# One decoder layer on one core: sums of u read from DRAM, and the order of the pooling pairs on TensorE

## The chip, the cores and the metric

The kernel runs on one core of one Trainium2 chip. Its time is the device time of one execution in microseconds. All work of the layer is in one program; nothing is computed on the host, which only lays out the weights in blocks.

## What is computed

512 tokens and 16 learned meta tokens in front of them (528 columns), model width 1024, one layer, float32. The normalised input goes through one wide projection. Its parts feed a pooling branch, an SSD branch (state-space scan, 8 groups of 4 heads) and two gates. The gated sum goes through `w_o`, then a squared-ReLU MLP, then a last norm.

```python
u = rmsnorm(h, mix_norm_w[i]); proj = u @ w_in[i]
u_pool, z, xbc, dt_raw, gates = ...                       # columns of proj
y_pool = pool_mixer(u_pool, pool_w_group[i], pool_scale[i]) @ w_pool_up[i]
y_ssd = mamba2_branch(z, xbc, dt_raw, ...) @ w_ssd_out[i]
h = h + (gate_pool * y_pool + gate_ssd * y_ssd) @ w_o[i]
hid = relu(rmsnorm(h, mlp_norm_w[i]) @ w_ff1[i]); h = h + (hid * hid) @ w_ff2[i]
...
def pool_mixer(u, w_group, scale):                        # windows 2, 4, 8, 16 for 4 groups of 256 channels
    ...
        mean = (cs - shifted) / count
        outs.append(mean.astype(u.dtype) - xg)
    y = einsum("blgc,gcd->blgd", stack(outs), w_group); return y * scale
```

## The kernel before

Every matrix is kept as a high part and a low part in the fp32r type, and a product takes three matmuls: high with high, high with low, low with high. ScalarE (ACT) casts the high part and VectorE (DVE) subtracts it to get the low part. For weights this is done per block of 128 x 1024: a load on the SyncE queue into `raw` (3 buffers), then `whi` and `wlo` (4 buffers each), at lines 82 and 83. So each 24 matmuls of width 512 on TensorE (PE) need one block from ACT and one from DVE.

The program is written as Python generators and placed by a planner: each engine executes a fixed queue in order, and the planner, which follows the traced order as priority, decides that queue ahead of time. `tc.issue_after(ins)` puts all instructions that are traced inside it, on the engine of `ins`, behind `ins` in that engine's queue.

**Start.** `norm_u` (line 375) scales the transposed input `xt[k]`, 8 tiles of 128 x 528, to u and splits it into `uh[k]` and `ul[k]`. Then the memory of `xt` is given up, and tiles of the SSD stage take it.

**SSD groups.** `weave` runs, for each g of 8, the scan `ssd(g)` step by step beside the projections of group g+1 (`group_proj`); in group 4 also `out_half`, whose products `pso` are copied from PSUM to `acc` by ACT at line 615. `ssd(g)` begins with `abc_load[g]`, a broadcast of 1 MB on GpSimd's (POOL's) DMA queue into the single buffer `abc`; ACT reads it first into `eb` (line 483). The mask is applied at line 522 (`masked[g]`), the squares are taken at line 546.

**Sums of u.** The projections of three pooling groups use a Strassen-like scheme on halves of K and of the tokens. It needs sums and differences of pieces of u. `sums_of_u(k, g)` (line 636) makes them for k = 0 to 3 in groups g = 1 to 4: POOL adds `uh + ul` for tiles k and k+4 into `ua` and `ub` (line 641), DVE combines them (lines 644 to 647), and for each of two results, "13" and "42", ACT casts `th` (line 651), DVE subtracts `tl` (line 652), and both are stored to DRAM, to the tensors `t_d13h`, `t_d13l`, `t_d42h` and `t_d42l`, on POOL's queue (lines 653, 654). `th` and `tl` have one buffer each, so the cast of "42" waits until the store of "13" has read `th`.

**Pooling.** After the groups, the first pooling group (3, window 16) is projected directly. The others (2, 1, 0, in this order; windows 8, 4, 2) are made by `pool_pair(p)`: four weight forms A, S, D and B are split (`split_form`, lines 100 and 101), and seven products of 12 matmuls of width 260 run in the order A into x, A into y, S into x, S into z, D into x, D into z, B into x. Between them ACT copies x and z out (lines 735, 739, 741, 749) and DVE adds y, x and z (737, 744, 746) into the two result tiles `pu`, of which there are 2 buffers. `averaged` (line 687) then takes the moving mean on DVE (lines 694, 696) and splits it into `ph` (line 700) and `pl` (701). `pool_mix` multiplies the two means of a pooling group by its 256 x 256 matrix: 12 matmuls of width 512 into two `pg` tiles, read out by lines 762 and 763. In PSUM x of all pairs lies in one tile of two banks, `pxx`, in alternating banks, and y and z in another one, `pyz`. `pool_pair` is a generator that stops after the fourth product; there `pool_mix` of the pooling group before it is traced, and then the other three products.

**After that** come the SSD gates (`pgs`), the up-projection (`pup`), `w_o` and the MLP, which the change does not touch.

Of the kernel before, what the change touches and what calls it, by code (L numbers as in the profile page):

```python
# [9 lines left out]
F32 = mybir.dt.float32  # L10
F32R = mybir.dt.float32r
AF = mybir.ActivationFunctionType
ALU = mybir.AluOpType

P = 128
# [3 lines left out]
L = SEQ + NM  # L19
HALF = L // 2  # L20
NK = D // P
# [20 lines left out]
POOL_ORDER = (3, 2, 1, 0)  # L42
# [4 lines left out]

SKIP = 8
TN = (L - SKIP) // 2


@with_exitstack
def kernel(ctx: ExitStack, tc, xT, x, w, vec, fnw, out):
    nc = tc.nc
    act, dve, pe, pool = nc.scalar, nc.vector, nc.tensor, nc.gpsimd
# [3 lines left out]
    dram = ctx.enter_context(tc.tile_pool(name="dram", bufs=1, space=bass.MemoryType.DRAM))  # L59
# [25 lines left out]
    def block():  # L85
        t = block_tiles()
        block_part(t, slice(0, 1024))
        return t[2:]
# [48 lines left out]
    def col(off, i, n=P):  # L137
        return vs[:n, off + i : off + i + 1]
# [10 lines left out]
    uh = [up.tile([P, 64 + SEQ], F32R, name=f"uh{k}")[:, 64 - NM :] for k in range(NK)]  # L149
    ul = [up.tile([P, 64 + SEQ], F32R, name=f"ul{k}")[:, 64 - NM :] for k in range(NK)]  # L150
# [6 lines left out]
    def psum2(name):  # L157
        return psa.tile([P, 1024], F32, tag="mm", name=name)
# [35 lines left out]
    xt = [pre.tile([P, L], F32, name=f"xt{k}") for k in range(NK)]  # L194
# [177 lines left out]
    act.activation(fl(cdec), pq[:, :128], AF.Exp)  # L372


    def norm_u():
        for k in range(NK):
            dve.scalar_tensor_tensor(xt[k], xt[k], col(V_MIX, k), rsb, op0=ALU.mult, op1=ALU.mult)
            act.copy(uh[k], xt[k])
            dve.tensor_tensor(ul[k], xt[k], uh[k].bitcast(F32), op=ALU.subtract)

# [59 lines left out]
    def ssd(g, cur):  # L440
# [71 lines left out]
        for c in range(3):  # L512
            pe.matmul(pv[c + 1], btok[:, c, :], xdd[:, c, :, :].rearrange("p r d -> p (r d)"),
                      start=True, stop=True)
        st0 = act.copy(flat(st[0]), pv[0])
        if g == G - 1:
            with tc.issue_after(st0.ins):
                decay()
# [24 lines left out]
            yield  # L543

        sq = gs.tile([P, 2, SEQ], F32, tag="eb", name=f"sqg{g}")
        act.activation(sq, yt, AF.Square)
        dve.tensor_tensor(sq[:, 0, :], sq[:, 0, :], sq[:, 1, :], op=ALU.add)
        qh, ql = col_sums(f"g{g}", sq[:, 0, :], gs, ("qh", "ql"))
        yield
# [15 lines left out]
            ys.append((yh, yl))  # L565
        yield

    done, abc_load, masked = {}, {}, {}

    def weave(a, b, n):  # L570

# [64 lines left out]
    def sums_of_u(k, g):  # L636
        a, b = (tsp.tile([P, 2 * TN], F32, tag=t, name=f"{t}{k}") for t in ("ua", "ub"))

        with tc.issue_after(abc_load[g].ins):
            for t, kk in ((a, k), (b, k + 4)):  # L640
                pool.tensor_tensor(t, uh[kk][:, SKIP:L].bitcast(F32), ul[kk][:, SKIP:L].bitcast(F32), op=ALU.add)
        yield
        with tc.issue_after(masked[g].ins):
            dve.tensor_tensor(a[:, one], a[:, two], a[:, one], op=ALU.subtract)
            dve.tensor_tensor(a[:, two], b[:, two], a[:, two], op=ALU.subtract)
            dve.tensor_tensor(b[:, two], b[:, two], a[:, one], op=ALU.subtract)
            dve.tensor_tensor(b[:, one], b[:, one], b[:, two], op=ALU.subtract)
        yield
        for src, n in ((a, "13"), (b, "42")):
            hi, lo = (tsp.tile([P, 2 * TN], F32R, tag=f"t{p}", name=f"t{p}{n}{k}") for p in "hl")  # L650
            act.copy(hi, src)
            dve.tensor_tensor(lo, src, hi.bitcast(F32), op=ALU.subtract)
            nc.gpsimd.dma_start(t_d[n, "h", k], hi)
            nc.gpsimd.dma_start(t_d[n, "l", k], lo)
            yield

    for g in range(G):
        nxt = group_tiles(g + 1) if g + 1 < G else None
        fill = [group_proj(g + 1, nxt, GATE_AT.get(g))] if nxt else [out_part()]
        if g == 4:  # L660
            fill = [out_half()] + fill
        if 0 < g < 5:
            fill.append(sums_of_u(g - 1, g))
        weave(ssd(g, cur), fill, 2 if g == 4 else 1)
        cur = nxt
    gc_stack.close()
# [5 lines left out]
    pool_stack = ExitStack()  # L672
    gp = pool_stack.enter_context(tc.tile_pool(name="gp", bufs=2, side="left", reuse_waits="tile"))
    tf = pool_stack.enter_context(tc.tile_pool(name="tf", bufs=1, side="left", reuse_waits="tile"))
    yps = {}

    def pool_tile(t):
        win = WIN[t // 2]
# [9 lines left out]
    def averaged(t, u):  # L688
        win = WIN[t // 2]
        s, wdt, lo_ = u, 1, min(NM - win, NM - 4)  # L690
        while wdt < win:
            o = gp.tile([P, L], F32, tag="pw", name=f"pw{t}_{wdt}")
            lo2 = lo_ + wdt
            dve.tensor_tensor(o[:, lo2:], s[:, lo2:], s[:, lo_ : L - wdt], op=ALU.add)
            s, lo_, wdt = o, lo2, 2 * wdt
        dve.scalar_tensor_tensor(s[:, NM:], s[:, NM:], 1.0 / win, u[:, NM:],
                                 op0=ALU.mult, op1=ALU.subtract)
        ph = gp.tile([P, SEQ], F32R, tag="ph", name=f"ph{t}", bufs=3)
        pl_ = gp.tile([P, SEQ], F32R, tag="pl", name=f"pl{t}", bufs=3)
        act.copy(ph, s[:, NM:])  # L700
        dve.tensor_tensor(pl_, s[:, NM:], ph.bitcast(F32), op=ALU.subtract)
        return ph, pl_

    def pool_pair(p):

        a1, a2 = raw_block(), raw_block()
        sm = tf.tile([P, 1024], F32, tag="sm", name=f"sm{p}")
        h1, h2, both = slice(0, 512), slice(512, 1024), slice(0, 1024)
        fa = split_form(a1, both, f"A{p}")
        dve.tensor_tensor(sm[:, h1], a2[:, h1], a2[:, h2], op=ALU.add)  # L710
        dve.tensor_tensor(sm[:, h2], sm[:, h1], a1[:, h1], op=ALU.subtract)
        fs = split_form(sm, both, f"S{p}")
        dve.tensor_tensor(a1[:, h1], a1[:, h1], a2[:, h1], op=ALU.subtract)
        dve.tensor_tensor(a1[:, h2], a1[:, h2], sm[:, h2], op=ALU.subtract)
        fd = split_form(a1, both, f"D{p}")
        fb = split_form(a2, h2, f"B{p}")
        r1, r2 = (gp.tile([P, L], F32, tag="pu", name=f"pu{2 * p + i}") for i in range(2))
        n = POOL_ORDER.index(p) % 2
        x, y, z = pxx[:, 512 * n : 512 * n + TN], pyz[:, :TN], pyz[:, 512 : 512 + TN]
        c1, c2 = slice(SKIP, SKIP + TN), slice(SKIP + TN, L)  # L720
        u1, u2 = (lambda k: (uh[k][:, c1], ul[k][:, c1])), (lambda k: (uh[k][:, c2], ul[k][:, c2]))
        form = lambda n, c: lambda k: (T[n, "h", k][:, c], T[n, "l", k][:, c])

        def product(ps, wf, c, f, start, stop, k0=0):
            for low in range(2):
                for k in range(4):
                    wt = wf[low][:, 512 * c + k * P : 512 * c + (k + 1) * P]
                    bh, bl = f(k0 + k)
                    pe.matmul(ps, wt, bh, start=start and not low and k == 0, stop=stop and low == 1 and k == 3,
                              skip_group_check=True)  # L730
                    if not low:
                        pe.matmul(ps, wt, bl, start=False, stop=False, skip_group_check=True)

        product(x, fa, 0, u1, True, False)
        act.copy(r1[:, c1], x)
        product(y, fa, 1, u1, True, True, 4)
        dve.tensor_tensor(r1[:, c1], r1[:, c1], y, op=ALU.add)
        product(x, fs, 1, form("42", two), False, False)
        act.copy(r1[:, c2], x)
        product(z, fs, 0, form("13", one), True, False)  # L740
        act.copy(r2[:, c2], z)
        yield
        product(x, fd, 0, form("13", two), False, False)
        dve.tensor_tensor(r2[:, c2], r2[:, c2], x, op=ALU.add)
        product(z, fd, 1, u2, False, True, 4)
        dve.tensor_tensor(r1[:, c2], r1[:, c2], z, op=ALU.add)
        first = averaged(2 * p, r1)
        product(x, fb, 1, form("42", one), False, True)
        act.copy(r2[:, c1], x)
        yield [first, averaged(2 * p + 1, r2)]  # L750

    def pool_mix(gi, pooled, wgb):
        ps = [psum1(f"pg{gi}_{j}") for j in range(2)]
# [29 lines left out]
        dve.tensor_tensor(acc[d], acc[d], ps, op=ALU.add)  # L783
    wgb = block()
    gate_pool(NK - 1)
    pxx, pyz = psum2("pxx"), psum2("pyz")
    for n, gi in enumerate(POOL_ORDER):
        if n < 3:
            pair = pool_pair(POOL_ORDER[n + 1])
            next(pair)  # L790
        if n == 3:
            gts = [gate_ssd(MERGE[0])]
        if n == 2:
            wgb = block()
        pool_mix(gi, pend, wgb)
        if n < 3:
            pend = next(pair)
    pool_stack.close()
    wo_stack = ExitStack()
    wop = wo_stack.enter_context(tc.tile_pool(name="wop", bufs=1, side="right", reuse_waits="tile"))  # L800
# [389 lines left out]
    for t in range(4):  # L1190
        T, st = t // 2, slice((t % 2) * P, (t % 2 + 1) * P)
        n = 0
# [27 lines left out]
def _weight_blocks(i):  # L1220
# [5 lines left out]
    def cols(m, c):  # L1226
        a = m[:, c : c + P]
        return a.reshape(NK, P, P).transpose(1, 0, 2).reshape(P, NK * P)

    def put(b):  # L1230
        blocks.append(b)
# [35 lines left out]
    wg(POOL_ORDER[0] // 2)  # L1267
    gate(NK - 1)
    for n in range(4):
        if n < 3:  # L1270
            for i in range(2):
                put(cols(w_in, (2 * POOL_ORDER[n + 1] + i) * P))
        if n == 3:
            gate(NK + MERGE[0])
        if n == 2:
            wg(POOL_ORDER[n] // 2)
# [78 lines left out]
```

## Time and profile before

| what | value |
|---|---|
| runs | 1027.02, 1026.06, 1026.90 us; median 1026.9 |
| the profiled execution | 1030.26 us, of which the span from first to last instruction is 1028.5 us |
| mean granted TensorE clock | 0.994 |
| PE busy | 1010.4 us (98%), 5661 matmuls |
| DVE busy | 773.1 us (75%) |
| ACT busy | 559.0 us (54%) |
| POOL busy | 38.7 us (4%), 64 instructions |
| DMA | 114.15 MB, mean 111 GB/s |

How to read rows of a timeline: start in us, duration in us, engine, line, operation, result<-inputs, shape, count of merged instructions; in brackets the idle time of the engine just before, and what ended it. `PEld` is the loading of weights into TensorE. A row of windows has, for each stretch, its length and then the busy time and count of PE, PEld, DVE, ACT and POOL, the granted clock, the DMA share and GB/s.

### The profile page before, as it was taken

How to read it: one execution, taken by the hardware profiler on the slowest of the kernel's cores; microseconds unless marked ns; L12 is line 12 of the kernel's file. 1: busy time of each engine (PE TensorE's matmuls, PEld its weight loads, DVE VectorE, ACT ScalarE, POOL GpSimd, SP SyncE). 2: the span in 40 equal slices, each digit the busy share in tenths (PEclk: the TensorE clock that was granted, in tenths of full speed). 3: DMA queues.
4: the chain of work that ended last, by engine and by line, in shares of the span. 5: the costliest groups of instructions: out<-in, count | busy, mean ns of one | idle time of the engine just before them, and what ended most of it. 6: DMA issues, size and time to landing. Idle time of an engine off the chain costs nothing. (4 is left out here: it accounts for less than half of the span.)

```text
span 1028.5 us, 14191 instructions
## 1 busy us (share of the span) xinstructions
PE 1010.4 (98%) x5661; PEld 869.4 (85%) x5661; DVE 773.1 (75%) x1039; ACT 559.0 (54%) x746; POOL 38.7 (4%) x64
## 2 busy tenths in 40 slices
PE   9999999999989999999989999999999999999997
PEld 8889899898879998978888888888888888888886
DVE  7978798978826676988868467877686686676866
ACT  7674958585727439573245333365545455454444
POOL 0101011202000000003000000000000000000000
PEclk9999999999989999999999999999999999999999
DMA  7242142615233321417223632224323323334112
GB/s 249 80 158 82 63 144 84 201 42 189 82 103 124 103 81 64 144 41 238 93 82 128 221 91 98 119 76 170 92 81 114 110 85 117 100 101 123 42 42 82
DMA packets 34322, 114.15 MB, mean 111 GB/s; under 512 B 3856, under 2 KB 5200, under 8 KB 33232
## 3 DMA queue, kind: packets, MB, share of 16 engines
q1 hardware_dynamic: 26928, 92.75, 28.5%
q0 software_dynamic: 6608, 19.60, 5.6%
q8 instruction: 44, 0.72, 0.3%
q10 hardware_dynamic: 720, 0.91, 0.2%
q14 instruction: 22, 0.18, 0.1%
HBM read 106.81 MB, written 6.42 MB: 110 GB/s over the span
## 5 line engine op out<-in xcount | busy, mean ns | idle before, releaser
L82 ACT CAST whi<-raw 128x1024 fp32r<-128x1024 f32 (+1 forms) x128 | 130.3, 1024 | 180.9 <-PE pf L115 47.0
L83 DVE TENSOR_TENSOR wlo<-raw,whi 128x1024 fp32r<-128x1024 f32 (+1 forms) x128 | 153.9, 1206 | 99.4 <-ACT whi L82 63.8
L178 PE MATMUL px<-uh,whi 128*128 128x264 f32 (+1 forms) x448 | 113.2, 291 | 0.0
L180 PE MATMUL px<-ul,whi 128*128 128x264 f32 (+1 forms) x448 | 110.3, 284 | 0.0
L114 PE MATMUL pf<-vh,whi 128*128 128x512 f32 x256 | 99.8, 390 | 0.0
L115 PE MATMUL pf<-vl,whi 128*128 128x512 f32 x256 | 99.6, 389 | 0.0
L178 PEld LDWEIGHTS px<-uh,whi 128*128 128x128 f32 x448 | 84.5, 189 | 2.0 <-issue 1.4
L180 PEld LDWEIGHTS px<-ul,whi 128*128 128x128 f32 x448 | 84.3, 188 | 0.3
L869 DVE TENSOR_TENSOR slo<-b,shi 128x1024 fp32r<-128x1024 f32 x35 | 42.7, 1219 | 28.8 <-ACT shi L868 15.2
L117 PE MATMUL pf<-vh,wlo 128*128 128x512 f32 x256 | 63.6, 389 | 0.0
L868 ACT CAST shi<-b 128x1024 fp32r<-128x1024 f32 x35 | 36.7, 1050 | 44.8 <-PE pf L115 30.2
L178 PE MATMUL px<-uh,wlo 128*128 128x264 f32 (+1 forms) x448 | 58.5, 283 | 0.0
L117 PEld LDWEIGHTS pf<-vh,wlo 128*128 128x128 f32 x256 | 48.0, 188 | 10.0
L114 PEld LDWEIGHTS pf<-vh,whi 128*128 128x128 f32 x256 | 48.1, 188 | 9.9
L115 PEld LDWEIGHTS pf<-vl,whi 128*128 128x128 f32 x256 | 48.0, 188 | 9.9
L178 PEld LDWEIGHTS px<-uh,wlo 128*128 128x128 f32 x448 | 55.9, 188 | 0.0
L1105 PE MATMUL alpha<-shi,hh 128*128 128x512 f32 x140 | 54.6, 390 | 0.0
L1108 PE MATMUL alpha<-shi,hl 128*128 128x512 f32 x140 | 54.5, 389 | 0.0
L935 DVE TENSOR_TENSOR ht<-ht,alpha 128x1024 f32<-128x1024 f32 x35 | 42.6, 1216 | 15.7 <-PE alpha L1105 15.7
L178 PE MATMUL pz<-uh,whi 128*128 128x512 f32 x112 | 43.9, 392 | 0.4 <-DVE xc L388 0.3
L180 PE MATMUL pz<-ul,whi 128*128 128x512 f32 x112 | 43.6, 390 | 0.0
L1105 PE MATMUL alpha<-slo,hh 128*128 128x512 f32 x140 | 37.4, 389 | 0.0
(494 smaller groups left out, 2413.3 us busy)
## 6 DMA issues: line engine op xcount, KB each, us to landing
raw<-in_w SPq DMA_DIRECT2D x128, 512.0 KB, 3.6
b<-in_w SPq DMA_DIRECT2D x28, 512.0 KB, 3.5
abc<-acs_d POOLq DMA_DIRECT2D x8, 1024.0 KB, 7.8
wob<-in_w SPq DMA_DIRECT2D x8, 512.0 KB, 5.0
xt<-in_xT SPq DMA_DIRECT2D x8, 264.0 KB, 4.9
ht<-in_x POOLq DMA_DIRECT2D x4, 512.0 KB, 5.8
w<-in_w SPq DMA_DIRECT2D x4, 512.0 KB, 3.6
out_dram<-out SPq DMA_DIRECT2D x4, 320.0 KB, 2.4
```

The source lines that it names most:

```text
L82: act.copy(hi[:, c], raw[:, c])
L83: dve.tensor_tensor(lo[:, c], raw[:, c], hi[:, c].bitcast(F32), op=ALU.subtract)
L114: pe.matmul(ps, ah, bh, start=first and n == 0, stop=False)
L115: pe.matmul(ps, ah, bl, start=False, stop=False)
L117: pe.matmul(ps, al, bh, start=False, stop=last and n == len(pairs) - 1)
L178: pe.matmul(o, wt, rhs[0][k][:, c], start=part == 0 and k == 0, stop=part == 1 and k == NK - 1)
L180: pe.matmul(o, wt, rhs[1][k][:, c], start=False, stop=False)
L868: act.copy(hi, src)
L869: dve.tensor_tensor(lo, src, hi.bitcast(F32), op=ALU.subtract)
L935: dve.tensor_tensor(o, o, src, op=op)
L1105: pe.matmul(ps[t], hh[:, p, seg, st], m, start=bool(first and not low and p == 0), stop=bool(last and low and p == 1), skip_group_check=True)
L1108: pe.matmul(ps[t], hl[:, p, seg, st], m, start=False, stop=False, skip_group_check=True)
```

## The change

Three things are changed. First, `norm_u` also stores each scaled `xt[k]` without its first 8 columns to DRAM (`u_d[k]`, 260 KB each, on POOL's queue), and `sums_of_u` loads `ua` and `ub` from there on the same queue in place of the two additions on POOL. Second, the sums are made in groups 1, 2, 3 and 5 and not 1 to 4; the cast of "13" is placed behind the first state copy of its group on ACT (`y_first`, line 515), the cast of "42" one step later and behind the squares (`squared`, line 546). Third, each pair gets its own x tile (a two-bank tile of which one bank is used) and y and z one-bank tiles of their own; `pool_pair` runs through without a stop, its products are chained in their traced order, and `pool_mix` of the second and third pooling group is placed on TensorE behind the last product of the next pair. The first `pool_mix` is traced ahead of the first pair. The order of the weight blocks in DRAM is written differently and comes out the same.

```diff
+SUMS_AT = (1, 2, 3, 5)
...
+    u_d = [dram.tile([P, 2 * TN], F32, name=f"u_d{k}") for k in range(NK)]
     def norm_u():
         for k in range(NK):
             dve.scalar_tensor_tensor(xt[k], xt[k], col(V_MIX, k), rsb, op0=ALU.mult, op1=ALU.mult)
+            nc.gpsimd.dma_start(u_d[k], xt[k][:, SKIP:])
             act.copy(uh[k], xt[k])
...
-        st0 = act.copy(flat(st[0]), pv[0])
+        y_first[g] = st0 = act.copy(flat(st[0]), pv[0])
...
-        act.activation(sq, yt, AF.Square)
+        squared[g] = act.activation(sq, yt, AF.Square)
...
         with tc.issue_after(abc_load[g].ins):
             for t, kk in ((a, k), (b, k + 4)):
-                pool.tensor_tensor(t, uh[kk][:, SKIP:L].bitcast(F32), ul[kk][:, SKIP:L].bitcast(F32), op=ALU.add)
+                nc.gpsimd.dma_start(t, u_d[kk])
...
         for src, n in ((a, "13"), (b, "42")):
             hi, lo = (tsp.tile([P, 2 * TN], F32R, tag=f"t{p}", name=f"t{p}{n}{k}") for p in "hl")
-            act.copy(hi, src)
+            if n == "42":
+                yield
+            with tc.issue_after((y_first if n == "13" else squared)[g].ins):
+                act.copy(hi, src)
...
-        if 0 < g < 5:
-            fill.append(sums_of_u(g - 1, g))
+        if g in SUMS_AT:
+            fill.append(sums_of_u(SUMS_AT.index(g), g))
...
     def pool_pair(p):
-        n = POOL_ORDER.index(p) % 2
-        x, y, z = pxx[:, 512 * n : 512 * n + TN], pyz[:, :TN], pyz[:, 512 : 512 + TN]
+        x = psum2(f"pxx{p}")[:, :TN]
+        y, z = (psum1(f"p{i}{p}")[:, :TN] for i in "yz")
...
-        def product(ps, wf, c, f, start, stop, k0=0):
+        def product(*a):
+            with tc.issue_after(last[p].ins) if p in last else nullcontext():
+                multiply(*a)
+
+        def multiply(ps, wf, c, f, start, stop, k0=0):
...
-                    pe.matmul(ps, wt, bh, ...)
+                    last[p] = pe.matmul(ps, wt, bh, ...)
...
         act.copy(r2[:, c2], z)
-        yield
         product(x, fd, 0, form("13", two), False, False)
...
-        yield [first, averaged(2 * p + 1, r2)]
+        return [first, averaged(2 * p + 1, r2)]
...
     for n, gi in enumerate(POOL_ORDER):
-        if n < 3:
-            pair = pool_pair(POOL_ORDER[n + 1])
-            next(pair)
+        if n == 0:
+            pool_mix(gi, pend, wgb)
+            nxt = pool_pair(POOL_ORDER[1])
+            continue
+        pend, nxt = nxt, pool_pair(POOL_ORDER[n + 1]) if n < 3 else None
+        if n == 2:
+            wgb = block()
         if n == 3:
             gts = [gate_ssd(MERGE[0])]
-        if n == 2:
-            wgb = block()
-        pool_mix(gi, pend, wgb)
-        if n < 3:
-            pend = next(pair)
+
+        with tc.issue_after(last[POOL_ORDER[n + 1]].ins) if n < 3 else nullcontext():
+            pool_mix(gi, pend, wgb)
```

More of the change, by code (lines that the diff above doesn't have):

```diff
@@ L566, in ssd @@
         yield
-    done, abc_load, masked = {}, {}, {}
+    done, abc_load, masked, y_first, squared = {}, {}, {}, {}, {}
     def weave(a, b, n):
@@ L674 @@
     tf = pool_stack.enter_context(tc.tile_pool(name="tf", bufs=1, side="left", reuse_waits="tile"))
-    yps = {}
+    yps, last = {}, {}
     def pool_tile(t):
@@ L728, in product @@
                     bh, bl = f(k0 + k)
-                    pe.matmul(ps, wt, bh, start=start and not low and k == 0, stop=stop and low == 1 and k == 3,
-                              skip_group_check=True)
+                    last[p] = pe.matmul(ps, wt, bh, start=start and not low and k == 0,
+                                        stop=stop and low == 1 and k == 3, skip_group_check=True)
                     if not low:
@@ L785 @@
     gate_pool(NK - 1)
-    pxx, pyz = psum2("pxx"), psum2("pyz")
     for n, gi in enumerate(POOL_ORDER):
-        if n < 3:
-            pair = pool_pair(POOL_ORDER[n + 1])
-            next(pair)
+        if n == 0:
[5 more added lines that the diff above has]
+            wgb = block()
         if n == 3:
             gts = [gate_ssd(MERGE[0])]
-        if n == 2:
-            wgb = block()
-        pool_mix(gi, pend, wgb)
-        if n < 3:
-            pend = next(pair)
+        with tc.issue_after(last[POOL_ORDER[n + 1]].ins) if n < 3 else nullcontext():
+            pool_mix(gi, pend, wgb)
     pool_stack.close()
@@ L1269, in _weight_blocks @@
     for n in range(4):
-        if n < 3:
+        for k in ((1, 2) if n == 0 else (n + 2,) if n == 1 else ()):
             for i in range(2):
-                put(cols(w_in, (2 * POOL_ORDER[n + 1] + i) * P))
+                put(cols(w_in, (2 * POOL_ORDER[k] + i) * P))
         if n == 3:
```

## The prediction

> **What bounds the kernel now.** I read the page's first section, then TensorE's list of waits, then the timeline around each wait.
>
> ```profile
> span 1028.5 us, 14191 instructions
> PE 1010.4 (98%) x5661; PEld 869.4 (85%) x5661; DVE 773.1 (75%) x1039; ACT 559.0 (54%) x746; POOL 38.7 (4%) x64
> ...
> PE pg L114 <- ACT ph L700: 4.1, 2, 2.8
> PE pso L114 <- ACT acc L615: 2.8, 1, 2.8
> ...
> PE ptx L470 <- DVE xdtm L463: 1.3, 1, 1.3
> ...
> PE pxx L729 <- ACT pu L749: 0.7, 1, 0.7
> ...
> PE pz L178 <- DVE xc L388: 0.3, 1, 0.3
> ```
>
> TensorE is busy 98% of the span and sets the end. The change leaves all 5661 matmuls as they are, so time can come only from TensorE's waits and from stretches at a lower clock. The waits in reach of the change are these rows: columns are total us, times, longest. I go through them by place.
>
> **Group 4: one cast of the sums.** First ACT and TensorE in order of time, then three windows (length; busy time of PE, PEld, DVE, ACT, POOL; granted clock).
>
> ```profile
> 285.80 0.62 ACT L651 CAST th<-ub 128x520 fp32r<-128x520 f32 x1 [3.23 <-DMA t_d13h<-th]
> 286.32 0.58 ACT L615 COPY acc<-pso 128x512 f32<-128x512 f32 x1
> ...
> 295.53 0.59 ACT L615 COPY acc<-pso 128x512 f32<-128x512 f32 x1 [0.78 <-PE pso L117]
> ...
> 281.27 1.98 PE L117 MATMUL pso<-yh,wlo 128*128 128x512 f32 x8
> 283.09 1.06 PE L529 MATMUL po<-ct,st 128*128 128x128 f32 x8
> 286.96 0.80 PE L114 MATMUL pso<-yh,whi 128*128 128x512 f32 x1 [2.81 <-ACT acc L615]
> ...
> 282.72:286.13 3.41, 1.42 (x11) 1.15 (x9) 1.83 (x2) 0.34 (x1) 0.00 (x0) 1.00 0.65 202
> 286.13:289.55 3.42, 2.59 (x6) 2.11 (x7) 0.70 (x1) 0.77 (x2) 1.06 (x2) 0.50 0.84 284
> 289.55:292.96 3.41, 3.41 (x9) 2.64 (x9) 0.00 (x0) 0.00 (x0) 0.00 (x0) 0.50 0.00 0
> ```
>
> The cast of "42" stood 3.23 us at the head of ACT's queue for the store of "13". The copy of `acc` behind it freed the PSUM tile that TensorE needed. TensorE idled 2.81 us, and then the clock was 0.50 over two windows with 2.59 + 3.41 us of work, of which half, 3.0 us, is loss: together 5.8 us. The change takes the sums out of group 4. What is late next there? The last `pso` of the tile ends at 281.27 + 1.98 = 283.25. In the row at 295.53 a free ACT waits for the product to end (0.78 us) and copies in 0.59 us, so here the copy would end near 283.9. TensorE has `po` until 283.09 + 1.06 = 284.15. Nothing is left: **-5.8 us** (a rest of 0.8 at most).
>
> [...]
>
> In group 5 the sums add two casts of 0.62 us on ACT and on DVE four operations of half width and two subtractions.
>
> ```profile
> 340.00:382.00 42.00, 42.00 (x313) 38.82 (x312) 27.77 (x38) 13.73 (x18) 0.00 (x0) 1.00 0.25 77
> ```
>
> In this stretch of group 5 TensorE idles nowhere, ACT works 13.73 of 42 us and DVE 27.77, so there is room. A group with sums did show one wait of 0.3 us (`pz`, group 2), and I take that as their price: **+0.3**, between 0 and the 5.8 that group 4 paid. The cast of "42" now stands behind the squares, so it should meet a store that is long done.
>
> **GpSimd's additions.** POOL, then DVE, the summary of that DVE line (min/median/max ns) and TensorE:
>
> ```profile
> 96.12 1.31 POOL L641 TENSOR_TENSOR ua<-uh,ul 128x520 f32<-128x520 f32 x1
> 97.39 1.32 POOL L641 TENSOR_TENSOR ub<-uh,ul 128x520 f32<-128x520 f32 x1
> ...
> 96.21 3.05 DVE L542 TENSOR_TENSOR yt<-yt,zt 128x512 f32<-128x512 f32 x1
> ...
> L542 DVE TENSOR_TENSOR yt<-yt,zt x16: 677/686/3053, 96.2 to 468.8; 128x512 f32<-128x512 f32 x16
> ...
> 115.61 0.66 PE L470 MATMUL ptx<-ident,xc 128*128 128x128 f32 x4 [1.29 <-DVE xdtm L463]
> ```
>
> A DVE product that takes 686 ns took 3053 while POOL added: DVE lost 2.37 us. It is the `yt` of the group whose squares, norm and transposes run up to 115.61, where TensorE waited 1.29 us for DVE. With the additions gone the chain is up to 2.37 us earlier, more than the wait: **-1.3** (0 if other links of the chain hold it).
>
> [...] If the cause were instead the 1 MB `abc` load of that moment, which stays, this term would be 0.
>
> **The new transfers.** Eight stores of 260 KB come into POOL's queue in `norm_u`, and eight loads in the place of the additions.
>
> ```profile
> abc<-acs_d POOLq DMA_DIRECT2D x8, 1024.0 KB, 7.8
> ...
> 61.56 0.76 DVE L377 SCALAR_TENSOR_TENSOR xt<-xt,vs,rsb 128x528 f32<-128x528 f32 x1
> ...
> 72.64 2.14 ACT L483 ACTIVATE eb<-abc 64x1024 f32<-64x1024 f32 x2
> ```
>
> The last `xt` is scaled at 62.3. Even at the 7.8 us that a transfer of four times the size takes, its store has landed by 70.1, and the first tile that reuses the memory is written at 72.64. They follow the first `abc` in POOL's queue and precede the second, which waits for group 0 anyway; no other engine's queue is touched. The loads into `ua` have most of a group before DVE reads them. Cost **0**; without that cover up to 7.8 us once.
>
> **The pairs.** TensorE, DVE, ACT, then two windows:
>
> ```profile
> 522.12 0.28 PE L729 MATMUL pyz<-t13h,whiS 128*128 128x260 f32 x1
> ...
> 523.54 0.28 PE L729 MATMUL pxx<-t13h,whiD 128*128 128x260 f32 x1
> ...
> 530.52 0.64 PE L729 MATMUL pyz<-uh,wloA 128*128 128x260 f32 x4
> 534.00 0.73 PE L114 MATMUL pg<-ph,whi 128*128 128x512 f32 x2 [2.83 <-ACT ph L700]
> ...
> 527.03 0.42 DVE L746 TENSOR_TENSOR pu<-pu,pyz 128x260 f32<-128x260 f32 x1
> ...
> 529.11 1.22 DVE L101 TENSOR_TENSOR wloD<-raw,whiD 128x1024 fp32r<-128x1024 f32 x1
> ...
> 532.60 0.69 DVE L696 SCALAR_TENSOR_TENSOR pw<-pw,pu 128x512 f32<-128x512 f32 x1
> ...
> 533.33 0.62 ACT L700 CAST ph<-pw 128x512 fp32r<-128x512 f32 x1 [2.42 <-DVE pw L696]
> 533.85 0.37 ACT L735 COPY pu<-pxx 128x260 f32<-128x260 f32 x1
> ...
> 550.88 0.72 PE L114 MATMUL pg<-ph,whi 128*128 128x512 f32 x2 [1.22 <-ACT ph L700]
> ...
> 531.89:535.30 3.41, 1.30 (x9) 1.22 (x10) 3.30 (x7) 0.89 (x2) 0.00 (x0) 1.00 0.70 249
> 535.30:538.71 3.41, 3.41 (x19) 3.41 (x17) 2.72 (x5) 0.53 (x2) 0.00 (x0) 0.50 0.10 38
> ```
>
> A product takes 523.54 - 522.12 = 1.42 us; a mix is 12 matmuls at (283.09 - 281.27)/8 = 0.23, so 2.7.
>
> *First boundary (pair 2 to pair 1).* TensorE ends the two A products at 531.16 and idles 2.83 us, then loses half of 3.41 us to the clock: 4.5 us. The named releaser is `ph`, for the mix. Putting the mix behind pair 1 takes this wait away, but another stands right behind it: S into x may not start before ACT's copy of x (line 735), and this copy needs a `pu` buffer, of which there are two, both pair 2's until DVE's line 696 has read them (532.60 + 0.69). The copy ends at 534.22, as late as `ph`. The change adds no `pu` buffer. DVE needs, after pair 2's sixth product, 0.42 for the add, four operations of 0.69 for window 8 and, between them by priority, splits of pair 1 (up to two of 1.22 and one of 0.69): 6.3 us, and ACT 1.0 more. TensorE has three products, 4.3 us. So the idle of about 3 us stays, with its clock: **0**. Behind it on ACT queue the later copies of x and z, and behind those TensorE.
>
> *Second boundary (pair 1 to pair 0).* Now B, the mix and both A products cover it: 3 x 1.42 + 2.7 = 7.0 us. DVE needs 0.42 + 3 x 0.69 (window 4) and the same splits, 5.6 us, and ACT 1.0: 6.6. So the 1.2 goes, and the 0.7, a wait of one pair's x for a copy out of the other pair's bank of `pxx`, goes with the own x tiles: **-1.9** (between +2.6, rival D, and -1.9). Moving the last mix behind pair 0 costs nothing: the gate product stands before it.
>
> **Sum.** -5.8 + 0.3 - 1.3 + 0 + 0 - 1.9 = -8.7 us. The profiled execution took 1030.26 us, 1.8 more than its span and 3.4 more than the median of the runs; it becomes 1021.6. The same waits are assumed in the runs: 1026.9 - 8.7 = **1018.2 us**.
>
> **The rivals.**
>
> *B, the clock stays up.* The two drops begin at 286.13 and 535.30, 249.17 us apart, 73 windows of 3.413; so windows stand on a fixed grid, and both were preceded by one with 2.0 and 2.1 us idle. If the wait at the first boundary falls across two windows in near halves, 1.7 us of clock is saved: 1016.5. Against: a wait of 3 us does so only in a quarter of all places.
>
> *C, the first boundary opens too.* If the planner puts DVE's averages before the splits, the need falls from 6.3 to 3.2 us, 4.2 with ACT, under the 4.3 of cover: another 4.5 us, 1013.7. Against: both kernels trace averages before splits, and the splits came between them all the same.
>
> *D, DVE limits the pairs.* One more split of 1.22 us in the second chain makes 7.8, over the cover of 7.0. The wait there can then become like the first, 4.5 us in place of 1.9: 2.6 more than before, 1022.7. For: DVE was busy 3.30 of 3.41 us in the window before 535.30.
>
> *E, the stall moves.* The sums stall in group 5 as they did in group 4: 1018.2 + 5.8 = 1024.0. Against: the cast behind the squares. That the DVE stretch is not POOL's would add 1.3.
>
> *F, slower: `abc` queued behind the stores.* POOL's queue is in order. Group 6's load and the first read of it:
>
> ```profile
> 382.07 0.54 POOL L448 DMA_DIRECT2D abc<-acs_d  x1 [71.59 <-DVE xc L388]
> ...
> 386.60 1.06 ACT L546 ACTIVATE sqg<-yt 128x1024 f32<-128x1024 f32 x1
> ...
> 393.57 1.06 ACT L483 ACTIVATE eb<-abc 64x1024 f32<-64x1024 f32 x1
> ```
>
> If the stores of "42", now behind the squares, stand ahead of the next `abc`, it is issued not at 382.07 but after squares, cast and subtraction (386.60 + 1.06 + 0.62 + 0.69) and two issues of 0.54, near 390.1. With 7.8 us to land it comes 4.3 us too late for ACT. In the four groups after a group with sums that is 17.2 us, if TensorE feels all of it: 1035.4. It makes the kernel slower once TensorE feels over 2.7 us per group. Against: `abc` is ready first, and the planner places by readiness.
>
> **How the numbers follow.** Forecast 0.46, B 0.13, C 0.13, D 0.12, E 0.08, F 0.08. The likeliest is 1018.2. The range 1012.8 to 1022.9 holds C, B, the forecast with its bounds and D, and leaves out E and F. A measurement of this kernel can tell about 0.2%, 2.1 us. Faster by more: all but F and a part of E and D, 0.87; same 0.05; slower 0.08.
>
> **What would show it.** Right: the waits list of the changed kernel has no `pso` from `acc` and no `ptx` from `xdtm`; line 542 has no 3 us instance; one clock drop is left, near the second pair, where TensorE waits for ACT's copy of x into `pu` and not for `ph`. Wrong: a wait of `pso` or `px` in group 5 behind `th`; the first boundary without a wait (C); two boundaries with one (D); `eb` waiting for the DMA of `abc` (F).

## The result, and the profile after

| kernel | median of the runs (us) | the kernel before beside it (us) | ratio, 95% interval | profiled execution (us) | its span (us) |
|---|---|---|---|---|---|
| changed, first chip | 1022.15 (1020.5 to 1022.98, 6 runs) | 1027.31 (6 runs) | 0.9943 (0.9928 to 0.9958) | 1022.45 | 1020.7 |
| changed, second chip | 1022.95 (1020.92 to 1024.2, 7 runs) | 1026.35 (18 runs) | 0.9969 (0.9956 to 0.9982) | 1020.92 | 1019.2 |

The change makes the kernel faster by 5.9 us on one chip and by 3.2 us on the other. Forecast were 1018.2 us, within 1012.8 to 1022.9, and faster. The first chip's 1022.15 lies 0.75 us under the top of that range, the second chip's 1022.95 just over it.

The page of the changed kernel, its head and the list of TensorE's waits (total us, times, longest):

```profile
span 1020.7 us, 14205 instructions
PE 1007.4 (99%) x5661; PEld 868.1 (85%) x5661; DVE 764.4 (75%) x1039; ACT 559.6 (55%) x746; POOL 36.0 (4%) x72
...
PE pxx L741 <- ACT pu L747: 3.0, 1, 3.0
PE po L534 <- DVE st L526: 1.7, 1, 1.7
...
PE psp L116 <- ACT yh L568: 0.4, 1, 0.4
PE ptx L475 <- DVE xdtm L468: 0.2, 1, 0.2
```

The waits of `pso` for `acc`, of `pg` for `ph` and of `pxx` for the other pair's bank are gone, and so are the 1.3 us of `ptx` for `xdtm`; the 0.2 us under that name stand in group 7. The wait of 3.0 us at the first boundary is there under the name that the prediction gave it. New, and not foreseen, is `po` for `st`.

**What went as forecast.** The summary of the DVE line that had an instance of 3053 ns (min/median/max ns), the stretch of group 5 (busy PE, PEld, DVE, ACT, POOL of 42 us), ACT in group 5, and then DVE, ACT and TensorE at the first boundary:

```profile
L547 DVE TENSOR_TENSOR yt<-yt,zt x16: 678/684/693, 96.8 to 463.2; 128x512 f32<-128x512 f32 x16
...
340.00:382.00 42.00, 42.00 (x316) 38.97 (x315) 29.36 (x45) 16.53 (x23) 2.17 (x4) 1.00 0.35 113
...
378.35 1.06 ACT L551 ACTIVATE sqg<-yt 128x1024 f32<-128x1024 f32 x1
379.31 0.61 ACT L659 CAST th<-ub 128x520 fp32r<-128x520 f32 x1
...
527.31 0.68 DVE L704 SCALAR_TENSOR_TENSOR pw<-pw,pu 128x512 f32<-128x512 f32 x1
...
528.55 0.37 ACT L747 COPY pu<-pxx 128x260 f32<-128x260 f32 x1
...
528.97 0.58 PE L741 MATMUL pxx<-t42h,whiS 128*128 128x260 f32 x1 [2.96 <-ACT pu L747]
```

No product of DVE is stretched any more. In group 5 TensorE works 42.00 of 42 us with the sums beside it, and the cast of "42" starts without a wait right behind the squares. At the first boundary DVE reads the last `pu` until 527.99. Only then may ACT copy x into that buffer; ACT casts `ph` first and copies at 528.55, and TensorE has waited 2.96 us when its product starts.

**What came new: group 7.** First TensorE, DVE and ACT of the changed kernel, then TensorE and ACT of the kernel before at the same place of the program:

```profile
443.13 0.38 PE L534 MATMUL po<-ct,st 128*128 128x128 f32 x2
445.18 0.49 PE L534 MATMUL po<-ct,st 128*128 128x128 f32 x2 [1.67 <-DVE st L526]
446.02 0.84 PE L116 MATMUL psp<-yh,whi 128*128 128x512 f32 x2 [0.35 <-ACT yh L568]
...
443.39 1.40 DVE L565 SCALAR_TENSOR_TENSOR yt<-yt,vs,rs 128x512 f32<-128x512 f32 x2
444.71 0.41 DVE L526 TENSOR_TENSOR st<-st,pst 128x256 f32<-128x256 f32 x1
...
444.42 1.04 ACT L500 ACTIVATE abc<-abc 128x1024 f32<-128x1024 f32 x1
445.37 1.12 ACT L568 CAST yh<-yt 128x512 fp32r<-128x512 f32 x2
```

```profile
450.57 0.39 PE L529 MATMUL po<-ct,st 128*128 128x128 f32 x2
451.81 0.73 PE L114 MATMUL psp<-yh,whi 128*128 128x512 f32 x2 [0.86 <-ACT yh L563]
452.38 0.39 PE L529 MATMUL po<-ct,st 128*128 128x128 f32 x2
...
451.16 0.60 ACT L563 CAST yh<-yt 128x512 fp32r<-128x512 f32 x1
451.67 1.06 ACT L495 ACTIVATE abc<-abc 128x1024 f32<-128x1024 f32 x1
```

In the kernel before, the planner put a cast of `yh` between the two halves of the decay on ACT, and on TensorE two products `psp` ahead of the second pair of `po`. In the changed kernel both halves come first on ACT, and `po` comes first on TensorE, where it waits for `st`, which stands behind two scalings of `yt` on DVE. 1.67 + 0.35 us of wait have taken the place of 0.86. No line of group 7 was edited.

### The profile page after: what moved, and what is told of

It is laid out like the page before. It is cut to its first block, busy times and chain, and to the rows that moved or that the text cites. A ratio compares the mean times of both kernels' runs of the same rounds, so it can differ in the third digit from the quotient of the medians.

```text
span 1020.7 us, 14205 instructions
## 1 busy us (share of the span) xinstructions
PE 1007.4 (99%) x5661; PEld 868.1 (85%) x5661; DVE 764.4 (75%) x1039; ACT 559.6 (55%) x746; POOL 36.0 (4%) x72
## 4 chain that ended last, share of the span: by engine, by line
PE 94%; DVE 3%; ACT 2%; issue 1%; DMA 1%; SPq 0%; ACTq 0%; DVEq 0%
PE px L180 11%; PE alpha L1117 6%; PE pf L116 6%; PE pf L117 6%; PE pf L119 6%; PE px L182 5%; PE pz L180 5%; PE alpha L1120 3%; PE pgp L180 3%; PE pgs L180 3%; PE pz L182 2%; PE py L540 2%; PE pso L116 2%; PE pgp L182 1%; PE wo_alpha L934 1%; PE pso L117 1%
## 5 line engine op out<-in xcount | busy, mean ns | idle before, releaser
L85 DVE TENSOR_TENSOR wlo<-raw,whi 128x1024 fp32r<-128x1024 f32 (+1 forms) x128 | 151.3, 1186 | 99.4 <-ACT whi L84 68.6
L561 DVE RECIPROCAL rs<-rs 128x128 f32<-128x128 f32 x32 | 27.2, 909 | 14.5 <-ACT rs L559 14.4
```

What stands on the lines that cost most here:

```text
L85: dve.tensor_tensor(lo[:, c], raw[:, c], hi[:, c].bitcast(F32), op=ALU.subtract)
```

## The experiments

Ratios are to runs of the kernel before on the same chip, with 95% intervals; 0.001 is 1.03 us.

### The first edit alone

```diff
 before.py
+    u_d = [dram.tile([P, 2 * TN], F32, name=f"u_d{k}") for k in range(NK)]
...
+            nc.gpsimd.dma_start(u_d[k], xt[k][:, SKIP:])
...
-                pool.tensor_tensor(t, uh[kk][:, SKIP:L].bitcast(F32), ul[kk][:, SKIP:L].bitcast(F32), op=ALU.add)
+                nc.gpsimd.dma_start(t, u_d[kk])
```

> The kernel before with the first edit alone: u stored in norm_u and loaded in sums_of_u in place of GpSimd's additions; groups 1 to 4, order of the casts and pairs as before. Theory (GpSimd's additions stretch the DVE product of that moment): no instance of the yt product over 0.8 us, the wait of ptx for xdtm (1.29 us) gone, the group 4 stall unchanged; 1.3 us less than before, ratio 0.9987. Rival 1 (the stretch comes from the load of abc, which stays): the 3 us products stay, ratio 1.0000. Rival 2 (the cast in group 4 waits because the additions come late): the pso wait goes too, 7.1 us less, ratio 0.993. Rival 3 (abc is issued late behind the stores): over 1.000, eb waits for the DMA of abc.

Measured: 0.9977 (0.9966 to 0.9987), 2.4 us less. No DVE product is stretched (681/687/693 ns), the `ptx` wait is gone. In this trace the group 4 wait is shorter too. ACT, then the wait list:

```profile
281.18 0.62 ACT L654 CAST th<-ub 128x520 fp32r<-128x520 f32 x1 [1.39 <-DMA t_d13h<-th]
...
PE pso L114 <- ACT acc L618: 1.0, 1, 1.0
```

The cast still waits for the store, 1.39 us and not 3.23: the store, issued at 276.48, had landed after 4.7 us; in the profile before it took 6.55 (279.25 to 285.80). The theory holds for `ptx`. The 2.4 us may hold a share of the shorter wait in group 4, so they are not the additions' price alone. Whether rival 2 has a share was still open here; the run without the second edit, below, settles it.

### The second edit alone

```diff
 before.py
+SUMS_AT = (1, 2, 3, 5)
...
-        st0 = act.copy(flat(st[0]), pv[0])
+        y_first[g] = st0 = act.copy(flat(st[0]), pv[0])
...
-        act.activation(sq, yt, AF.Square)
+        squared[g] = act.activation(sq, yt, AF.Square)
...
-            act.copy(hi, src)
+            if n == "42":
+                yield
+            with tc.issue_after((y_first if n == "13" else squared)[g].ins):
+                act.copy(hi, src)
...
-        if 0 < g < 5:
-            fill.append(sums_of_u(g - 1, g))
+        if g in SUMS_AT:
+            fill.append(sums_of_u(SUMS_AT.index(g), g))
```

> The kernel before with the second edit alone: groups 1, 2, 3, 5 and the casts placed behind the state copy and the squares; GpSimd's additions and the pairs as before. Theory (this edit takes the group 4 stall, 5.8 us, and makes the new wait of po for st in group 7: 1.67 + 0.35 us in place of a psp wait of 0.86, and 1.7 us of clock, together 2.9): a pso wait of 2.8 us gone, a po wait of about 1.7 us there, the ptx wait of 1.3 us still there; 2.9 us less than before, ratio 0.997. Rival 1 (the po wait comes from the loads of u, or from the pairs): no po wait, 5.8 us less, ratio 0.994. Rival 2 (group 5 stalls in its turn with the additions there): a pso, px or pz wait of 3 us in group 5, ratio 1.000.

Measured: 1.0004 (0.9993 to 1.0016): no gain, and so not the theory's 0.997 but the 1.000 of rival 2. The `po` wait of 1.7 us is there, so this edit makes it. The stall of "42" is gone, but GpSimd's additions for group 5 now make another `pso` wait, of 1.41 us where the rival had 3. POOL, DVE, ACT and TensorE at the end of group 4:

```profile
304.39 1.31 POOL L643 TENSOR_TENSOR ua<-uh,ul 128x520 f32<-128x520 f32 x1
305.66 1.32 POOL L643 TENSOR_TENSOR ub<-uh,ul 128x520 f32<-128x520 f32 x1
...
304.46 3.08 DVE L542 SCALAR_TENSOR_TENSOR yt<-xc,vs,yt 128x512 f32<-128x512 f32 x1
...
308.29 1.06 ACT L548 ACTIVATE sqg<-yt 128x1024 f32<-128x1024 f32 x1 [5.16 <-DVE yt L544]
...
310.71 0.57 ACT L617 COPY acc<-pso 128x512 f32<-128x512 f32 x1
...
311.34 0.50 PE L116 MATMUL pso<-yh,whi 128*128 128x512 f32 x1 [1.41 <-ACT acc L617]
```

A DVE operation whose median is 744 ns took 3.08 us beside the additions of 1.31 and 1.32, the squares came late, and the copy of `acc` behind them. So the second edit needs the first: with u from DRAM this wait does not arise.

### The third edit alone

```diff
 before.py
-        n = POOL_ORDER.index(p) % 2
-        x, y, z = pxx[:, 512 * n : 512 * n + TN], pyz[:, :TN], pyz[:, 512 : 512 + TN]
+        x = psum2(f"pxx{p}")[:, :TN]
+        y, z = (psum1(f"p{i}{p}")[:, :TN] for i in "yz")
...
-        pool_mix(gi, pend, wgb)
+        with tc.issue_after(last[POOL_ORDER[n + 1]].ins) if n < 3 else nullcontext():
+            pool_mix(gi, pend, wgb)
```

> The kernel before with the third edit alone: own PSUM tiles per pair and the mix behind the next pair; sums as before. Theory (the two pu buffers hold the first boundary, the mix held the second): at the first boundary a wait of about 3 us, now of pxx for the copy into pu, with its clock; the 1.22 and 0.7 us waits at the second gone; 1.9 us less than before, ratio 0.998. Rival 1 (the mix was all that held the first boundary): no wait there, 6.4 us less, ratio 0.994. Rival 2 (DVE limits the pairs): the second boundary waits 3 us, 2.6 us more, ratio 1.0025.

Measured: 0.9973 (0.996 to 0.9986), 2.8 us less, against 1.9 expected. The list has one wait left at the pairs:

```profile
PE pxx L733 <- ACT pu L739: 3.0, 1, 3.0
PE pso L114 <- ACT acc L615: 2.6, 1, 2.6
```

The theory holds: the second boundary is free, the first waits as long as before, under another name. The interval has room for 1.9.

### The changed kernel without the two rules for the casts

```diff
 after.py
-            if n == "42":
-                yield
-            with tc.issue_after((y_first if n == "13" else squared)[g].ins):
-                act.copy(hi, src)
+            act.copy(hi, src)
```

> The changed kernel without the two rules that place the casts of the sums on ACT behind the state copy and behind the squares; the groups 1, 2, 3, 5 stay. The built order of group 7 is then that of the kernel before on TensorE, ACT and DVE. Theory (the rules make the planner order group 7 so that po waits for st; they aren't needed for the group 5 sums): no po wait, no pso wait, 2.9 us less than the changed kernel, near 0.9915 of the kernel before. Rival (the rules are what spares group 5 the stall of group 4): the cast of 42 waits about 3 us for the store of 13 in group 5 and TensorE with it, 5.8 us more against 2.9 less: 2.9 us more than the changed kernel, 0.997 of the kernel before.

Measured: 0.9927 (0.9911 to 0.9944). TensorE's waits:

```profile
PE pxx L738 <- ACT pu L744: 3.0, 1, 3.0
...
PE psp L116 <- ACT yh L568: 0.9, 1, 0.9
```

No `po` wait and none in group 5; the old 0.9 of `psp` is back. ACT's two casts in group 5:

```profile
362.21 0.63 ACT L656 CAST th<-ua 128x520 fp32r<-128x520 f32 x1 [0.30 <-DVE ua L650]
371.42 0.61 ACT L656 CAST th<-ub 128x520 fp32r<-128x520 f32 x1
```

They stand 9.2 us apart, more than the 4.7 to 6.63 us in which the store of group 4 landed in three traces, and the second waits for nothing: the rules are not needed in group 5. The median, 1019.24, is 2.9 us under the changed kernel's 1022.15, though on another chip.

### The sums in groups 1 to 4, the rules kept

```diff
 after.py
-SUMS_AT = (1, 2, 3, 5)
+SUMS_AT = (1, 2, 3, 4)
```

> The changed kernel with the sums in groups 1 to 4 and the two rules for the casts kept. The order of group 7 is that of the kernel before. Theory (the place of the cast behind the squares is enough, the move to group 5 isn't needed): no wait of pso over 0.5 us in group 4, no po wait, 0.9927 of the kernel before. Rival (the projection tiles of group 4 are too short of cover, wherever the cast stands): a pso wait of 1 to 3 us with its clock, 0.995 to 0.997.

Measured: 0.9913 (0.9897 to 0.993), better than the changed kernel's 0.9943 (0.9928 to 0.9958) on another chip; the intervals overlap by 0.0002. ACT in group 4, then the wait list:

```profile
303.58 1.06 ACT L551 ACTIVATE sqg<-yt 128x1024 f32<-128x1024 f32 x1 [2.84 <-DVE yt L547]
304.54 0.61 ACT L659 CAST th<-ub 128x520 fp32r<-128x520 f32 x1
...
PE pxx L741 <- ACT pu L747: 3.0, 1, 3.0
...
PE psp L116 <- ACT yh L568: 0.9, 1, 0.9
```

In the kernel before this cast stood ahead of a copy of `acc` in group 4; now it stands behind the squares, TensorE has no wait in group 4, and group 7 keeps its old order. So neither the rules alone nor the move to group 5 alone reorders group 7, but both together do. The move to group 5 is not needed, and with the rules it costs.

### The first and the third edit without the second

> The first and the third edit without the second: u from DRAM, the pairs, and the sums in groups 1 to 4 with their old order. Theory (the group 4 stall is the landing of the store of 13, which has nothing to do with GpSimd's additions): a pso wait between 1 and 3 us in group 4, its length with the landing; 0.9977 and 0.9973 together, 0.995 of the kernel before, 2.3 us more than without the rules. Rival (the additions were what made group 4 late): pso wait under 0.5 us, as without the rules, 0.9927.

```diff
 after.py
-SUMS_AT = (1, 2, 3, 5)
...
-            if n == "42":
-                yield
-            with tc.issue_after((y_first if n == "13" else squared)[g].ins):
-                act.copy(hi, src)
+            act.copy(hi, src)
...
-        if g in SUMS_AT:
-            fill.append(sums_of_u(SUMS_AT.index(g), g))
+        if 0 < g < 5:
+            fill.append(sums_of_u(g - 1, g))
```

Measured: 0.995 (0.9931 to 0.9969). ACT, then the list:

```profile
282.64 0.62 ACT L654 CAST th<-ub 128x520 fp32r<-128x520 f32 x1 [3.30 <-DMA t_d13h<-th]
...
PE pso L114 <- ACT acc L618: 2.9, 1, 2.9
```

No additions by GpSimd are in this kernel, and the stall has its full length, 2.9 us. So the landing of the store sets it, and the rival is out. Beside the run above (0.9913, the same chip), whose trace has the same order on TensorE, the stall is worth 3.8 us here.

### The kernel before with the two rules and nothing else

```diff
 before.py
+            if n == "42":
+                yield
+            with tc.issue_after((y_first if n == "13" else squared)[g].ins):
+                act.copy(hi, src)
-            act.copy(hi, src)
```

> The kernel before with nothing but the two rules for the casts, sums in groups 1 to 4. TensorE's order is that of before; on ACT the cast of 42 of group 4 stands nine instructions later, behind the squares, and its subtraction on DVE with it. Theory (the place of this one cast was the whole group 4 stall): the pso wait of 2.8 us gone, the ptx and the pair waits as before; 2.8 us of wait and 0 to 3.4 us of clock less than before, ratio 0.995 to 0.997. Rival (with GpSimd's additions in group 4 something else stalls it): pso wait of over 1 us, 0.999 to 1.000.

Measured: 0.9977 (0.9967 to 0.9988), 2.4 us less (1.2 to 3.4). TensorE's longest wait and one of 1.3, then ACT's cast of "42" in group 4:

```profile
PE pg L116 <- ACT ph L705: 4.0, 2, 2.8
...
PE ptx L472 <- DVE xdtm L465: 1.3, 1, 1.3
...
307.56 0.61 ACT L656 CAST th<-ub 128x520 fp32r<-128x520 f32 x1
```

The `pso` wait is gone and all the long ones stand. The order on TensorE is that of the kernel before. On ACT the cast of group 4 stands eight places later, on DVE its subtraction has moved with it, and one cast of weights changes places near 315 us; the rest is in the old order. So one cast, moved eight places on ACT, is the whole of the group 4 stall, and its worth over many executions is 2.4 us where the prediction's profile gave 5.8. The ratio is just over the 0.995 to 0.997 that the theory expected, with 0.997 inside the interval.

### The changed kernel once more

The kernel is the changed one, with no edit.

> The changed kernel once more, on the chip of the other two runs of this call, so that the versions are compared with one set of runs of before. Both theories: 0.9943 of the kernel before, po wait of 1.67 us in group 7, pxx wait of 2.96 us at the first boundary; the clock falls behind each where a window on the 3.41 us grid holds 1.5 us of idle or more, and not where it holds 1.3 or less. Rival (the clock falls only after a window that is idle throughout): no drop behind waits of this length.

Measured: 0.9969 (0.9956 to 0.9982). The waits are the same to 0.01 us (1.68 `po`, 0.34 `psp`, 2.96 `pxx`), but the clock fell only behind the last: it was 0.50 from 527.34, after a stretch in which TensorE was busy 0.46 of 3.42 us. Two windows (length; busy PE, PEld, DVE, ACT, POOL; clock) of this run, then of the first run:

```profile
442.00:445.41 3.41, 1.72 (x9) 1.19 (x7) 3.41 (x7) 3.40 (x4) 0.00 (x0) 1.00 0.00 0
445.41:448.83 3.42, 3.08 (x12) 2.28 (x13) 3.15 (x5) 1.87 (x3) 0.00 (x0) 1.00 0.00 0
```

```profile
443.07:446.49 3.42, 1.40 (x7) 0.80 (x6) 3.15 (x7) 3.41 (x5) 0.00 (x0) 1.00 0.00 0
446.49:449.90 3.41, 3.41 (x10) 2.48 (x8) 3.34 (x4) 1.04 (x2) 0.00 (x0) 0.50 0.00 0
```

Both pairs of windows are laid in steps of 3.413 us from a drop of their own trace (527.34 and 446.49). Here TensorE idled 1.69 us in the first window and 0.34 in the second, and the clock stayed 1.00; in the first run both waits of group 7 lie in the first window, with 2.02 us of idle, and the clock was 0.50 in the second. So the 1.5 us in the expectation did not hold. Neither did its rival: ahead of the two drops TensorE was busy 1.40 and 0.46 of 3.42 us.

### Three `pu` buffers

```diff
 after.py
-        r1, r2 = (gp.tile([P, L], F32, tag="pu", name=f"pu{2 * p + i}") for i in range(2))
+        r1, r2 = (gp.tile([P, L], F32, tag="pu", name=f"pu{2 * p + i}", bufs=3) for i in range(2))
...
-        u = gp.tile([P, L], F32, tag="pu", name=f"pu{t}")
+        u = gp.tile([P, L], F32, tag="pu", name=f"pu{t}", bufs=3)
```

> The changed kernel with three pu buffers in place of two. Theory (the first boundary waits because the copy of x needs a pu tile that the moving mean of the pair before still reads): the wait of pxx for pu, 2.96 us, goes, and the clock loss behind it, 1.7 us in the profile; 3.0 to 4.7 us less than the changed kernel, 0.990 of the kernel before. Rival (DVE is the limit there, 6.3 us of work against 4.3 of cover): the wait only moves on, to a later product that waits for the forms of weights or for an addition into pu, or to the mix, 2 to 3 us long; no difference, 0.994.

Measured: 0.9935 (0.9918 to 0.9953), median 1020.5. The wait list, DVE at the second boundary, and the windows over both boundaries, this kernel's and then the changed kernel's:

```profile
PE pxx L741 <- ACT whiD L102: 1.5, 1, 1.5
...
541.35 0.69 DVE L722 TENSOR_TENSOR raw<-raw,sm 128x512 f32<-128x512 f32 x1
...
525.00:544.00 19.00, 17.47 (x133) 16.61 (x132) 18.69 (x31) 9.68 (x17) 0.00 (x0) 1.00 0.18 56
```

```profile
525.00:544.00 19.00, 16.04 (x113) 15.31 (x112) 17.54 (x28) 9.97 (x16) 0.00 (x0) 0.91 0.27 82
```

Both sides were right in part; the ratio is nearer to the rival's 0.994 than to the theory's 0.990. The wait for `pu` is gone, which shows that the two buffers made it. 1.5 us of it come back behind the second boundary, where TensorE waits for the form D, whose difference DVE makes at 541.35: DVE is busy 18.69 of 19 us. With this wait the clock did not fall.

### Three `pu` buffers, without the rules, and with the sums in groups 1 to 4

Both have the edit of three buffers. The first of them also has this one:

```diff
 after.py
-            if n == "42":
-                yield
-            with tc.issue_after((y_first if n == "13" else squared)[g].ins):
-                act.copy(hi, src)
+            act.copy(hi, src)
```

> The changed kernel without the two rules for the casts and with three pu buffers. Theory: both waits that were left, po for st in group 7 and pxx for pu, are gone, 0.9927 less 3.0 to 4.7 us, so 0.988 to 0.990 of the kernel before. Rival (DVE limits the pairs): as without the third buffer, 0.9927.

And the second this one:

```diff
 after.py
-SUMS_AT = (1, 2, 3, 5)
+SUMS_AT = (1, 2, 3, 4)
```

> The changed kernel with the sums in groups 1 to 4, the two rules kept, and three pu buffers. Theory (the effects are independent: the group move costs 2 to 3 us, the pu buffer 1.5 to 3): no po wait, no pxx wait for pu, a pxx wait of 1.5 us for whiD at the second boundary; 0.9913 less 0.0015 to 0.003, so 0.988 to 0.990 of the kernel before. Rival (what the third buffer saves comes back as DVE work at the second boundary): 0.991.

Measured: 0.9904 (0.9887 to 0.9921), median 1017.23, and 0.9909 (0.9895 to 0.9922), median 1016.84. Beside the same kernels with two buffers (0.9927 and 0.9913) the third buffer is worth 2.4 and 0.4 us, with intervals that overlap. The second has these waits:

```profile
PE pxx L741 <- ACT whiD L102: 1.5, 1, 1.5
...
PE psp L116 <- ACT yh L568: 0.9, 1, 0.9
```

The second comes out at its rival's 0.991 and not at 0.988 to 0.990: most of what the third buffer saves there comes back. The first lies between its theory and its rival. It ran on the same chip as the kernel with three buffers alone, and the runs of the two do not overlap (1016.37 to 1017.96 and 1018.21 to 1021.77). So taking the rules away saves 3.2 us there (0.9935 to 0.9904), which prices the new wait of group 7 with its clock.

Both beat the changed kernel: 1022.95 against 1016.84 on one chip.

## Why the prediction was right, and where it was not

| step | forecast (us) | the profile after | the runs (us) |
|---|---|---|---|
| group 4 stall | -5.8 | wait of 2.81 and both slow windows gone | -2.4 alone; -3.8 beside the first and third edits |
| sums in group 5 | +0.3 | 0; but +1.16 of wait in group 7, and 1.7 of clock in one of two traces | +3.2 for group 7, with three `pu` buffers |
| GpSimd's additions | -1.3 | 1.29 gone | -2.4 alone (-1.3 to -3.5) |
| transfers | 0 | no wait of TensorE | |
| first boundary | 0 | 2.96 for 2.83, one slow window as before | |
| second boundary | -1.9 | 0.73 and 1.22 gone | -2.8 with the first boundary (-1.4 to -4.1) |

**The sum against the profile** was nearly right: -8.7 forecast, and the span fell from 1028.5 to 1020.7, by 7.8. Every wait that it named went or stayed as it said. Its sign of one clock drop left did not hold: there are two, since group 7 took back 1.16 us of wait and a slow window (1.7 us). Against that stand the 0.3 us that group 5 didn't cost and the 0.3 us of `pz` that went too. In the page's totals, TensorE's idle time fell by 4.8 us (18.1 to 13.3) and its busy time by 3.0. Of the 3.0, 1.6 is clock: half of the 2.59 + 3.41 + 3.41 us that TensorE worked in slow windows before, less half of 3.41 + 2.85 after. Some 1.4 us of the busy time is not resolved, and without them the sum would be further off; that it came so near is in part luck.

**The step that failed** is the last of the sum: "The same waits are assumed in the runs: 1026.9 - 8.7". The waits of the two traces of the changed kernel agree to 0.01 us; the clock loss behind them does not. The profiled execution of before took 1030.26 us, more than any of the 64 timed runs of that kernel (1023.87 to 1029.91). Its stall in group 4 went on for 0.83 us after the clock fell (286.13 to 286.96), and the clock was 0.50 over two windows, which cost 3.0 us. The traces of other kernels with the same stall have 2.58 and 2.89 us of wait with one slow window each (1.7 us), and 0.97 us with none; this wait hangs on the landing of a store, and is not itself the same each time. So the term of 5.8 was the dear end: 2.4 to 3.8 are what it is worth in the runs. With that alone the forecast would have been 1020.2 to 1021.6. In the runs the other terms are larger than forecast too: -2.4 for the first edit (-1.3), -2.8 for the third (-1.9), and +3.2 for the new wait in group 7 (+0.3). With group 4 they add up to -4.4 to -5.8 us, against -5.9 and -3.2 measured.

**Luck.** That 1022.15 fell inside the range is in part luck. Its top was set by rival D with 1022.7, to which the measured time is nearer than to the forecast, and D did not come; the wait in group 7, which took its place, stood in no rival.

**The transfers** cost TensorE nothing, as forecast, but not in the order that the prediction had. It put the eight stores behind the first `abc` in POOL's queue; in the trace they stand ahead of it, and `abc` is issued at 63.77 us, where the kernel before issued it at 50.36. ACT reads it at 75.35, so 11.6 us lie between, and TensorE works without a gap from 60.6 to 80.6.

**The cause of the new wait** is shown in part. The rules with sums in group 5 make it; either without the other doesn't. In the traces, the changed kernel and the one without the rules have the same order on ACT and DVE up to the cast of "42" in group 5 and its subtraction. The cast starts at 379.31 with the rules and at 371.42 without, and from there on operations change places, through group 6 into group 7. What in the planner's reckoning carries this on to group 7 is not shown.

**The rivals.** B (the clock stays up behind the wait at the first boundary) came in neither of the two traces of the changed kernel. It does happen: in the kernel with the sums in groups 1 to 4, whose trace has its only drop there, two of six runs have a mean clock of 1.000 and 1016.8 and 1016.86 us, the other four 0.997 or 0.998 and 1017.94 to 1019.24; a slow window by itself takes 0.0017 off the mean (1.7 of 1017 us). Two of the first six runs of the changed kernel have 0.998 and 1020.5 and 1021.26 us, the other four 0.995 or 0.996 and 1022.04 to 1022.98; which of the two drops is missing there is not known. C did not happen; D came only with the third `pu` buffer, where DVE is busy 18.69 of 19 us, and at 1.5 us. E did not happen in group 5. F did not: ACT waited 0.3 us, once, for the DMA of `abc`.

## What to carry to other kernels

When the head of an in-order queue waits for a transfer, as ACT did for 3.23 us in the kernel before, ask what can stand ahead of it: moving one cast by eight places was worth 2.4 us, about as much as each of the other edits (2.4 and 2.8), and moving the work to another group was not needed. Cost a wait in two parts, the wait itself, which here repeated to a few hundredths where engines set it and not where the landing of a store did, and the clock behind it, which after the same waits in group 7 was 0.50 for 3.41 us in one trace of the changed kernel and 1.00 in the other; take the second from several executions and not from one that is slower than all the others. And when a planner places the program, compare the built order of the engines in stages that were not edited: the loss was in group 7.

## What the runs showed of the hardware

The two drops of the clock to 0.50 in the kernel before start 249.17 us apart, 73 times 3.413; those of the changed kernel, at 446.49 and 528.41, 81.92 us apart, 24 times 3.413. The clock came back after 3.41 us in three of these four and after 6.83 us in group 4 of the kernel before. TensorE had idled 1.99 and 2.11 us in the 3.41 us ahead of the drops of the kernel before, 2.02 and 2.40 us ahead of those of the changed kernel, and 2.96 us ahead of the one in its second trace. After the 1.69 us in the window from 442.00 of that second trace there was no drop.

The store of "13" in group 4, 260 KB to DRAM, had landed 4.7 us after its issue in the run of the first edit, 6.55 us in the kernel before and 6.63 us in the run of the first and third edit; what set the difference was not tried.
